# Product sums of the down weights made in device memory: one encoder layer on one core

## The chip, the cores and the metric

One core of a Trainium2 chip runs the kernel. The metric is the device time of one execution in microseconds (us). The engines are TensorE (PE, with its weight loads as PEld), VectorE (DVE), ScalarE (ACT), GpSimd (POOL) and SyncE (SP, which here only issues transfers). Transfers (DMA) run on 16 DMA engines that all the queues share.

## What is computed

One layer of a hybrid encoder over 512 positions of width 1024, float32, cut to what matters:

```python
h  = rmsnorm(x, g_pre_mix)
q, k, v, g, u, sv, a_ret, a_sgu = split(h @ w_in)         # 512, 512 and six times 1024 wide
merged = sigmoid(a_ret) * retention(q, k, v, g) @ w_ret_o \
       + sigmoid(a_sgu) * sgu(u, sv) @ w_sgu_o
x1 = x + rmsnorm(merged @ w_out, g_post_mix)
h2 = rmsnorm(x1, g_pre_ffn)
a, b = split(conv3(h2 @ w_up))                            # 2 x 2816 wide
y  = x1 + rmsnorm((gelu(a) * b) @ w_down, g_post_ffn)     # w_down: 2816 x 1024
```

The last line holds what the change touches: the product with `w_down`, called the down stage, and what follows it, called the tail.

## The kernel before

Every matrix product is done as three matmuls. An operand is split into a high part (a copy on ACT that rounds, line 103, in `copy`) and a low part (source minus high part, a subtraction on DVE, line 123, in `split`), and high x high, high x low and low x high are summed. All weights lie in `wall`, 146 blocks of 128 x 1024, in the order of use. SP loads them into `raw` tiles (four of them, 128 x 1024); split parts go to nine slots of their own. `w_get` takes the next piece of the list `units` and issues loads and splits up to a fixed amount ahead of the matmuls; beyond that, the order on each engine comes from a scheduler that places an instruction when its inputs are due. Each engine runs its own list strictly in order, and an instruction that waits holds all that stands behind it. That holds for transfers too: the engine that issues one waits for its inputs first.

Many products are done in a form of Strassen's scheme, with seven block products in place of eight. They need sums of blocks of the weights and of the other operand. In the down stage, 18 of the 22 row blocks of `w_down` are taken as nine pairs (j = 0 to 8), the other four as they are ("whole"). In a first phase each pair needs four products, with the operand's forms A11, S2, S1 and A22, in a second phase three (A12, S4, S3); each has two token tiles and three matmuls, at line 1406 in `product`. The whole blocks have line 1418. Per pair the weights come from two blocks, a = `wall[i]` and b = `wall[i+1]`, each of two halves C1 and C2 (512 columns), in `w_down`:

- `da` loads a and adds C1 to C2 in place (by DVE at line 236 for even j, by an adding transfer that GpSimd issues, line 234, for odd j). It gives two products.
- `d2` loads b's C2 and adds the sum of `da` (line 244), `d4` loads b's C1 and adds the sum of `d2` (line 247). Each gives one product; their tiles are `dr`, their parts `dt`.
- In the second phase `dc` loads b, and `dd` loads a's C2 and adds b's C2 (line 241).

The operand's forms are made as the gated products `gp` come out of the up stage (`tile_done`), but those of four pairs (`LATE`) only inside the down stage, by `down_sums`, `down_parts` and `down_rest`. Their low parts are made by `split_added`: high part on ACT, its negative on ACT (line 1286), and an adding transfer from GpSimd (line 1287).

In the tail each of four token tiles needs the sum of its squares (ACT, line 1461, into `junk`), a scale from it (DVE at 1472, then GpSimd at 1473), a product with the gain `gpf` (`weighted`, line 1468), a multiply-add with x1 (`rows`, line 1484) and stores (`stored`, line 1477, which takes SP and ACT in turn). For token tiles 0 and 2, `rows_added` (line 1490) scales on DVE and adds x1 by an adding transfer from GpSimd (line 1491) before the store. For tiles 1 and 3 x1 is loaded by SP.

The mixing half of the layer matters here through GpSimd's list: each of four retention heads has a short chain on GpSimd (`rs` line 478, `orstd` line 481, `oshift` line 742), for whose result ACT waits at line 745.

Of the kernel before, what the change touches and what calls it, by code (L numbers as in the profile page):

```python
# [10 lines left out]
F32 = mybir.dt.float32  # L11
# [44 lines left out]
def tile_block(ctx: ExitStack, tc, xT, x, wall, par, cs, wsp, bsp, gpost, gffn, out):  # L56
# [42 lines left out]
    def const(n, shape):  # L99
        return sb.tile(list(shape), F32, tag=n, bufs=1, name=n)  # L100

    def copy(o, i):
        return nc.scalar.activation(out=o, in_=i, func=AF.Copy)  # L103

    def two(t):
        return t.rearrange("p (n c) -> p n c", n=2)
# [8 lines left out]
    def as32(t):  # L115
        return t.bitcast(F32)

    low, w_load = [None], [None]
    HALVES = slice(0, S), slice(S, 2 * S)

    def split(hi, lo, src):
        copy(hi, src)
        low[0] = nc.vector.tensor_sub(lo, src, as32(hi)).ins  # L123


# [6 lines left out]
    while i < NW:  # L132
        pair = [(f, i) for f in FORMS]
        if i == SV0:
            units += [(f, k) for f in ("s11", "sT1", "sT2") for k in range(2)]
            units += [(f, k) for k in range(2) for f in ("s22", "sT3")]
            units += [(f, k) for f in ("s21", "sT4") for k in range(2)]
            i = U0
        elif i == U0:
            us, gs = ([[(f, k + n * m) for f in FORMS] for n in range(KD // 2)] for k, m in ((U0, 2), (GATE0, 4)))  # L140
            ws = [("blk", GATE0 + 4 * (n // 2) + 2 + n % 2) for n in range(KD)]
            for what, n in MIDDLE:
                units += {"W": lambda: ws[n : n + 1], "U1": lambda: us[n][:4], "U2": lambda: us[n][4:],
                          "G1": lambda: gs[n][:4], "G2": lambda: gs[n][4:]}.get(what, list)()
# [77 lines left out]
    def w_down(form, j):  # L222

        i = DOWN0 + 2 * j
        c1, c2 = HALVES

        def load(o, n, c=slice(0, 1024)):
            nc.sync.dma_start(o, wall[i + n, :, c])
            return o

        if form in ("da", "dc"):
            raw = w_raw["a"] = load(raw_tile(), form == "dc")
            if form == "da" and j % 2:
                nc.gpsimd.dma_start(raw[:, c2], wall[i, :, c1], accum_op=ALU.add)
            elif form == "da":
                nc.vector.tensor_add(raw[:, c2], raw[:, c1], raw[:, c2])
            hi, lo = slot("dh", AT_192), slot("dl", AT_192)
        else:
            if form == "dd":
                raw = load(blk(n="dr"), 0, c2)  # L240
                nc.vector.tensor_add(raw, raw, w_raw["a"][:, c2])
            elif form == "d2":
                raw = w_raw["t"] = load(blk(n="dr"), 1, c2)
                nc.vector.tensor_add(raw, w_raw["a"][:, c2], raw)
            else:
                raw = load(blk(n="dr"), 1, c1)
                nc.vector.tensor_add(raw, w_raw["t"], raw)
# [3 lines left out]
        return hi, lo  # L251

    s_sum, s_22 = {}, {}

    def w_sv(form, kp):
# [38 lines left out]
        return w_block(u[1]) if u[0] == "blk" else (w_down if u[0][0] == "d" else w_sv if u[0][0] == "s" else w_form)(*u)  # L294

    def w_size(u):
        return 2 if u[0] in ("blk", "da", "dc") or u[0][0] == "s" else 1

    def w_get(look=LOOK):

# [985 lines left out]
        nc.scalar.activation(out=lo, in_=as32(hi), func=AF.Copy, scale=-1.0)  # L1286
        nc.gpsimd.dma_start(lo, src, accum_op=ALU.add)  # L1287

    def two_parts(t):
        h_, l_ = blk(F32R, "fh"), blk(F32R, "fl")  # L1290
        split_added(h_, l_, t)
        return h_, l_

    firsts, whole, raws = [], [], {}
# [135 lines left out]
    for j in range(DP):  # L1430
        end = j == DP - 1
        if j in LATE:
            n = FORMED + LATE.index(j)
            if n == DP - 1:
                down_sums(n, True)
# [38 lines left out]
        return sc  # L1474

    def stored(n, t, a, b, o):
        (nc.sync, nc.scalar)[n % 2].dma_start(out[t, :, a:b], o)  # L1477

    def rows(t, sc, which, pieces=((0, 512), (512, 1024))):
        for n, (a, b) in enumerate(pieces):  # L1480
# [6 lines left out]
    def rows_added(t, sc, srcs):  # L1487
        for i, src in enumerate(srcs):
            o = blk(n="zs")
            pin(v.scalar_tensor_tensor(out=o, in0=src, scalar=sc, in1=gpf[i], op0=ALU.mult, op1=ALU.mult))  # L1490
            nc.gpsimd.dma_start(o, x1[t][i], accum_op=ALU.add)  # L1491
            stored(i, t, i * S, (i + 1) * S, o)

    yy = halves("e")
    pin = tc.keep_in_program_order
    for j in range(DP):
# [7 lines left out]
            for i in range(2):  # L1504
                nc.gpsimd.dma_start(gpf[i], gffn[None, i * S : (i + 1) * S].to_broadcast([P, S]))
        if j < len(LATE):
            down_rest(FORMED + j)
# [33 lines left out]
    pin(v.tensor_sub(uu[1], m5[1], uu[1]))  # L1541
    square(1, 1, uu[1])
# [140 lines left out]
```

## Time and profile before

| | |
|---|---|
| median of 3 runs | 797.47 us (797.26 to 798.8) |
| profiled execution | 796.85 us, span in the trace 795.1 us |
| granted TensorE clock, mean | 0.989 |
| first matmul of the down stage | 673.6 us |
| first matmul of the whole blocks at the end | 765.25 us |
| last matmul ends | 781.05 us |

The page gives busy times per engine, and the span in 40 slices; the rows of the slices show TensorE at nine tenths or more everywhere but in three places, the second half of the span's last fifth:

```profile
PE   9999999999999999999999999999999999979992
PEclk9999999999999999999999999999999999989997
```

"Idle before" an instruction, in square brackets in a timeline, is the time its engine waited, with what ended the wait. A row of windows has the length, then the busy time of each engine, the granted clock, the DMA engines' busy share and GB/s.

### The profile page before, as it was taken

Reading aid. Unit: us, or ns where it says so; the run is one execution under the profiler, and the core shown is the slowest. Engines: PE = TensorE matmul, PEld = TensorE weight load, DVE = VectorE, ACT = ScalarE, POOL = GpSimd, SP = SyncE. Lnnn points to the kernel's source line nnn. Section 1 sums busy time; section 2 is a strip of 40 time slices with the busy share of each in tenths; the row PEclk is TensorE's granted clock in tenths of the full one; section 3 lists DMA queues with packets and bytes.
Section 4 is the critical chain, followed back from the end, with each engine's and each line's share of the span. In section 5 each row is a group of like instructions: output and inputs, shape, how many; then the busy total and the mean of one; then the engine's idle time right before and its main releaser. Section 6 shows DMA issues by size and latency. Waiting matters only on the chain. (4 is left out here: it accounts for less than half of the span.)

```text
span 795.1 us, 12585 instructions
## 1 busy us (share of the span) xinstructions
PE 772.2 (97%) x4677; PEld 704.8 (89%) x4677; DVE 627.5 (79%) x1050; ACT 492.2 (62%) x884; POOL 117.4 (15%) x147
## 2 busy tenths in 40 slices
PE   9999999999999999999999999999999999979992
PEld 7888999998999999999988999999999998867882
DVE  7467878789789987877765689889999986857764
ACT  7655657788467765644544685657777755646531
POOL 0040010130101102122111200002111102210011
PEclk9999999999999999999999999999999999989997
DMA  8872224462232332333656122335555559886835
GB/s 292 297 221 83 84 76 160 107 153 99 80 111 76 111 128 80 107 106 106 198 197 242 54 80 75 111 113 146 140 146 147 146 164 230 225 219 224 245 93 149
DMA packets 41645, 115.74 MB, mean 146 GB/s; under 512 B 5040, under 2 KB 6960, under 8 KB 41584
## 3 DMA queue, kind: packets, MB, share of 16 engines
q1 hardware_dynamic: 31536, 94.89, 36.2%
q0 software_dynamic: 9184, 18.88, 11.9%
q10 hardware_dynamic: 864, 1.18, 0.4%
q8 instruction: 36, 0.59, 0.3%
q14 instruction: 25, 0.20, 0.1%
HBM read 100.51 MB, written 4.19 MB: 132 GB/s over the span
## 5 line engine op out<-in xcount | busy, mean ns | idle before, releaser
L123 DVE TENSOR_TENSOR wl<-raw,wh 128x1024 fp32r<-128x1024 f32 (+1 forms) x86 | 100.4, 1177 | 59.4 <-issue 20.5
L103 ACT ACTIVATE wf<-raw 128x512 fp32r<-128x512 f32 x140 | 85.9, 625 | 67.0 <-issue 25.5
L945 PE MATMUL ps<-sh,wf 128*128 128x256 f32 x640 | 117.2, 276 | 0.1
L123 DVE TENSOR_TENSOR wf<-raw,wf 128x512 fp32r<-128x512 f32 x140 | 104.9, 755 | 10.1 <-ACT wf L103 9.7
L103 ACT ACTIVATE wh<-raw 128x1024 fp32r<-128x1024 f32 (+2 forms) x90 | 87.1, 981 | 37.3 <-DMA raw<-wall 12.8
L945 PEld LDWEIGHTS ps<-sh,wf 128*128 128x128 f32 x640 | 102.0, 192 | 0.9 <-ACT sig L103 0.5
L320 PE MATMUL ps<-h2h,wh 128*128 128x512 f32 (+1 forms) x256 | 90.6, 354 | 0.0
L321 PE MATMUL ps<-h2l,wh 128*128 128x512 f32 (+1 forms) x256 | 90.4, 353 | 0.0
L322 PE MATMUL ps<-h2h,wl 128*128 128x512 f32 (+1 forms) x256 | 90.4, 353 | 0.0
L945 PE MATMUL ps<-sl,wf 128*128 128x256 f32 x320 | 88.0, 275 | 0.0
L945 PEld LDWEIGHTS ps<-sl,wf 128*128 128x128 f32 x320 | 61.4, 192 | 0.4
L322 PEld LDWEIGHTS ps<-h2h,wl 128*128 128x128 f32 x256 | 48.6, 190 | 5.1
L320 PEld LDWEIGHTS ps<-h2h,wh 128*128 128x128 f32 x256 | 48.6, 190 | 4.5
L321 PEld LDWEIGHTS ps<-h2l,wh 128*128 128x128 f32 x256 | 48.6, 190 | 4.5
L945 PE MATMUL ps<-xh,wf 128*128 128x256 f32 x288 | 52.2, 275 | 0.0
L655 PE MATMUL ps<-wh,xl 128*128 128x512 f32 x128 | 48.5, 379 | 0.0
L654 PE MATMUL ps<-wl,xh 128*128 128x512 f32 x128 | 48.5, 379 | 0.0
L653 PE MATMUL ps<-wh,xh 128*128 128x512 f32 x128 | 48.5, 380 | 0.0
L945 PEld LDWEIGHTS ps<-xh,wf 128*128 128x128 f32 x288 | 45.6, 192 | 0.2
L1287 POOL DMA_DIRECT2D fl<-gp x26 | 23.1, 960 | 125.3 <-DVE wl L123 63.6
L945 PE MATMUL ps<-xl,wf 128*128 128x256 f32 x144 | 39.6, 275 | 0.0
L945 PE MATMUL ps<-h2h,wf 128*128 128x256 f32 x192 | 34.7, 275 | 0.0
(348 smaller groups left out, 2073.1 us busy)
## 6 DMA issues: line engine op xcount, KB each, us to landing
raw<-wall SPq DMA_DIRECT2D x146, 512.0 KB, 3.7
dr<-wall SPq DMA_DIRECT2D x27, 256.0 KB, 6.2
x<-x SPq DMA_DIRECT2D x20, 256.0 KB, 6.3
fl<-gp POOLq DMA_DIRECT2D x18, 256.0 KB, 5.2
fl<-fs POOLq DMA_DIRECT2D x9, 256.0 KB, 4.6
swap<-qkraw POOLq DMA_DIRECT2D x16, 128.0 KB, 4.5
x<-x POOLq DMA_DIRECT2D x8, 256.0 KB, 2.3
xT<-xT SPq DMA_DIRECT2D x7, 256.0 KB, 4.4
```

What stands on the lines that cost most here:

```text
L103: return nc.scalar.activation(out=o, in_=i, func=AF.Copy)
L123: low[0] = nc.vector.tensor_sub(lo, src, as32(hi)).ins
L320: nc.tensor.matmul(o, ah, bh, start=start, stop=False, skip_group_check=skip)
L321: nc.tensor.matmul(o, ah, bl, start=False, stop=False, skip_group_check=skip)
L322: pe_last[0] = nc.tensor.matmul(o, al, bh, start=False, stop=stop, skip_group_check=skip).ins
L653: nc.tensor.matmul(acc[t], xh[k][:, c], turns(wh[:, f]), start=k == 0, stop=False)
L654: nc.tensor.matmul(acc[t], xh[k][:, c], turns(wl[:, f]), start=False, stop=False)
L655: part_end[0] = nc.tensor.matmul(acc[t], xl[k][:, c], turns(wh[:, f]), start=False, stop=k == KD - 1)
L945: self.last = nc.tensor.matmul(o, w_[:, c], a_, start=first and k == n == 0, stop=k == 3 and n == 2, skip_group_check=True,)
L1287: nc.gpsimd.dma_start(lo, src, accum_op=ALU.add)
```

## The change

For each pair j three tensors in device memory are added: t42 (128 x 1024), t1 and t3 (128 x 512). They get the sums that `da`, `d2`, `d4` and `dd` made on chip: t1 = a.C1 + a.C2, t42's C2 = b.C2 + t1, t42's C1 = b.C1 + that, t3 = a.C2 + b.C2. Each begins as a copy from device memory to device memory, issued by ACT (27 in all), to which GpSimd's adding transfers add (36 in all). These 63 operations are issued while other stages run: `copy` counts its calls, and at the counts in `SUMS_AT` it issues the next one behind that copy; an adding transfer waits for that copy, and for the transfers whose results it reads or adds to. Counts 29 to 140 hold the first 48 operations, 312 to 345 the last 15.

`w_down` then only loads: `da` is a.C1 and t1 (two loads into one raw tile), `db` is t42 (one raw tile, two products), `dc` is b as before, `dd` is t3. The 27 sums on DVE and four adding transfers go. In `units`, `d2` and `d4` become one `db` of size 2.

For the late pairs `parted` uses `split`, so their low parts are DVE subtractions (12) in place of 12 negative copies on ACT and 12 adding transfers; these forms are issued after the latest weight split on ACT and DVE (`w_split`). In the tail, tile 0 is done as tile 1 is: `weighted` and `rows`, with x1 loaded by SP; `stored` uses ACT only for tiles above 0, and the second store of tile 2 goes to SP.

```diff
+SUMS_AT = [a + k * (b - a) // n for a, b, n in ((29, 67, 28), (72, 100, 6), (106, 140, 14), (312, 345, 15)) for k in range(n)]
...
     def copy(o, i):
-        return nc.scalar.activation(out=o, in_=i, func=AF.Copy)
+        done = nc.scalar.activation(out=o, in_=i, func=AF.Copy)
+        copies[0] += 1
+        while sums_at and copies[0] >= sums_at[0]:
+            sums_at.pop(0)
+            sums_ops.pop(0)(done.ins)
+        return done
...
+    def sums_copy(j, n):
+        def op(after):
+            i = DOWN0 + 2 * j
+            with tc.issue_after(after):
+                nc.scalar.dma_start(sums[j][n], (wall[i + 1], wall[i, :, C2], wall[i, :, C2])[n])
+        return op
+
+    def sums_add(j, n):
+        def op(after):
+            (t42, t1, t3), i = sums[j], DOWN0 + 2 * j
+            o, src = ((t1, wall[i, :, C1]), (t42[:, C2], t1), (t3, wall[i + 1, :, C2]), (t42[:, C1], t42[:, C2]))[n]
+            add = tc.keep_in_program_order(nc.gpsimd.dma_start(o, src, accum_op=ALU.add))
+            tc.add_manual_dep(
+                add.ins, after.name, mybir.DependencyInfo(mybir.DependencyClass.Sync, mybir.DependencyReason.DATA),
+                reason="paced",
+            )
+        return op
+
+    sums_ops, ended_ = [], []
+    for js in [range(j, min(j + 2, DP)) for j in range(0, DP, 2)]:
+        sums_ops += [sums_copy(j, n) for n in (1, 0) for j in js] + ended_
+        for j in js:
+            sums_ops += [sums_add(j, 0), sums_copy(j, 2)]
+        sums_ops += [sums_add(j, 1) for j in js] + [sums_add(j, 2) for j in js]
+        ended_ = [sums_add(j, 3) for j in js]
+    sums_ops += ended_
...
-                units += [("da", j), ("d2", j), ("d4", j)]
+                units += [("da", j), ("db", j)]
...
     def w_down(form, j):
...
+        t42, t1, t3 = sums[j]
+        if form == "dd":
+            raw = blk(n="dr")
+            nc.sync.dma_start(raw, t3)
             w = slot("dt", 0, 1088)
             lo, hi = w[:, AT_64 : AT_64 + S], w[:, S + AT_192 : 2 * S + AT_192]
+        else:
+            raw = raw_tile()
+            if form == "da":
+                nc.sync.dma_start(raw[:, C1], wall[i, :, C1])
+                nc.sync.dma_start(raw[:, C2], t1)
+            else:
+                nc.sync.dma_start(raw, t42 if form == "db" else wall[i + 1])
+            hi, lo = slot("dh", AT_192), slot("dl", AT_192)
         split(hi, lo, raw)
+        w_split[:] = high[0], low[0]
         return hi, lo
...
     def parted(j, t, *names):
-        h_, l_ = two_parts(t)
+        h_, l_ = two_parts(t, split if j >= FORMED else split_added)
...
-            down_parts(n)
+            with tc.issue_after(w_split[0]), tc.issue_after(w_split[1]):
+                if n == DP - 1:
+                    down_sums(n, True)
+                down_parts(n)
...
-        product(m6, w_get(), 0, "S2", j, last=None)
+        wb = w_get()
+        product(m6, wb, 1, "S2", j, last=None)
...
-        product(m4, w_get(), 0, "A22", j, None)
+        product(m4, wb, 0, "A22", j, None)
...
-        (nc.sync, nc.scalar)[n % 2].dma_start(out[t, :, a:b], o)
+        (nc.sync, nc.scalar)[n % 2 and t > 0].dma_start(out[t, :, a:b], o)
...
-            stored(i, t, i * S, (i + 1) * S, o)
+            nc.sync.dma_start(out[t, :, i * S : (i + 1) * S], o)
...
-        for t in (1, 3):
+        for t in (0, 1, 3):
...
+    weighted(0, 0, m1[0])
...
+    weighted(0, 1, uu[0])
...
-    rows_added(0, s0, (m1[0], uu[0]))
+    rows(0, s0, (0, 1))
```

The change moves instructions in three places. The first is DVE's order inside the first phase of the down stage, before and after (a row has the line, the operation, output and inputs, and the shape; the numbers in names only count tiles). Line 123 of before is line 165 of the change.

```order
L244 TENSOR_TENSOR dr_7666<-raw_7653,dr_7666 128x512
L247 TENSOR_TENSOR dr_7684<-dr_7666,dr_7684 128x512
L244 TENSOR_TENSOR dr_7709<-raw_7696,dr_7709 128x512
L123 TENSOR_TENSOR dl_7657<-raw_7653,dh_7656 128x1024
L247 TENSOR_TENSOR dr_7727<-dr_7709,dr_7727 128x512
L123 TENSOR_TENSOR fa_7792<-gp_7406,fa_7792 128x256
L123 TENSOR_TENSOR dt_7669<-dr_7666,dt_7669 128x512
L123 TENSOR_TENSOR dt_7687<-dr_7684,dt_7687 128x512
```
```order
L165 TENSOR_TENSOR dl_7686<-raw_7683,dh_7685 128x1024
L165 TENSOR_TENSOR fl_7708<-fs_7191,fh_7707 128x512
L165 TENSOR_TENSOR fl_7712<-gp_7186,fh_7711 128x512
L165 TENSOR_TENSOR dl_7719<-raw_7715,dh_7718 128x1024
L165 TENSOR_TENSOR dl_7731<-raw_7728,dh_7730 128x1024
L165 TENSOR_TENSOR dl_7756<-raw_7752,dh_7755 128x1024
```

Before, three sums (L244 and L247, of this pair and the next) stand ahead of the split `dl_7657`; now splits follow one another, with the low parts `fl` of a late form between them.

The second is the end of ACT's order, before and after (line 1461 is 1496 of the change, 1477 is 1512).

```order
L1461 ACTIVATE junk_8329,q_7980<-ps_7533 128x512
L1461 ACTIVATE junk_8352,q_7980<-c_7541 128x512
L1477 DMA out<-zs_8335 128x512
L1461 ACTIVATE junk_8370,q_7981<-ps_7534 128x512
L1461 ACTIVATE junk_8395,q_7981<-c_7542 128x512
L1461 ACTIVATE junk_8416,q_7983<-e_7985 128x256
L1477 DMA out<-zs_8378 128x512
L1461 ACTIVATE junk_8437,q_7983<-e_7985 128x256
```
```order
L1496 ACTIVATE junk_8348,q_8006<-ps_7611 128x512
L1496 ACTIVATE junk_8373,q_8006<-c_7619 128x512
L1496 ACTIVATE junk_8393,q_8007<-ps_7612 128x512
L1496 ACTIVATE junk_8414,q_8007<-c_7620 128x512
L1496 ACTIVATE junk_8435,q_8009<-e_8011 128x256
L1496 ACTIVATE junk_8456,q_8009<-e_8011 128x256
L1512 DMA out<-zs_8420 128x512
L1512 DMA out<-zs_8437 128x256
```

Two stores that stood between the squares now go elsewhere, and the stores that stay on ACT come after the last square.

The third is GpSimd's order around the first retention heads, before and after (478 is 511, 481 is 514, 742 is 775 of the change; line 131 is the adding transfer of `sums_add`).

```order
L478 TENSOR_SCALAR rs_985<-mv 128x4
L481 TENSOR_TENSOR orstd<-rs_985,nhalf 128x4
L742 TENSOR_TENSOR oshift<-oshift,orstd 128x4
L478 TENSOR_SCALAR rs_1273<-mv 128x4
L481 TENSOR_TENSOR orstd<-rs_1273,nhalf 128x4
L742 TENSOR_TENSOR oshift<-oshift,orstd 128x4
```
```order
L511 TENSOR_SCALAR rs_1026<-mv 128x4
L514 TENSOR_TENSOR orstd<-rs_1026,nhalf 128x4
L775 TENSOR_TENSOR oshift<-oshift,orstd 128x4
L131 DMA sum_0_63<-sum_0_63 128x512
L131 DMA sum_0_66<-sum_0_66 128x512
L131 DMA sum_1_70<-wall 128x512
L131 DMA sum_1_73<-wall 128x512
L131 DMA sum_0_69<-sum_1_70 128x512
L131 DMA sum_0_72<-sum_1_73 128x512
L511 TENSOR_SCALAR rs_1325<-mv 128x4
```

Between one head's chain and the next now stand six adding transfers; the last two add results of the two before them (`sum_0` is t42, `sum_1` is t1 and `sum_2` is t3).

More of the change, by code (lines that the diff above doesn't have):

```diff
@@ L100, in const @@
         return sb.tile(list(shape), F32, tag=n, bufs=1, name=n)
+    copies, sums_at = [0], list(SUMS_AT)
     def copy(o, i):
-        return nc.scalar.activation(out=o, in_=i, func=AF.Copy)
+        done = nc.scalar.activation(out=o, in_=i, func=AF.Copy)
[4 more added lines that the diff above has]
+        return done
+    C1, C2 = slice(0, S), slice(S, 2 * S)
+    sums = [[
+        dp_.tile([P, w * S], F32, tag=f"sum{j}_{n}", name=f"sum{j}_{n}") for n, w in enumerate((2, 1, 1))
+    ] for j in range(DP)]
+    def sums_copy(j, n):
[22 more added lines that the diff above has]
+    sums_ops += ended_
     def two(t):
@@ L116, in as32 @@
         return t.bitcast(F32)
-    low, w_load = [None], [None]
+    low, high, w_load = [None], [None], [None]
     HALVES = slice(0, S), slice(S, 2 * S)
     def split(hi, lo, src):
-        copy(hi, src)
+        high[0] = copy(hi, src).ins
         low[0] = nc.vector.tensor_sub(lo, src, as32(hi)).ins
@@ L224, in w_down @@
         i = DOWN0 + 2 * j
[L225 to L247, printed above, removed]
+        t42, t1, t3 = sums[j]
+        if form == "dd":
+            raw = blk(n="dr")
+            nc.sync.dma_start(raw, t3)
             w = slot("dt", 0, 1088)
             lo, hi = w[:, AT_64 : AT_64 + S], w[:, S + AT_192 : 2 * S + AT_192]
+        else:
[6 more added lines that the diff above has]
+            hi, lo = slot("dh", AT_192), slot("dl", AT_192)
         split(hi, lo, raw)
+        w_split[:] = high[0], low[0]
         return hi, lo
+    w_split = []
     s_sum, s_22 = {}, {}
@@ L296, in w_size @@
     def w_size(u):
-        return 2 if u[0] in ("blk", "da", "dc") or u[0][0] == "s" else 1
+        return 2 if u[0] in ("blk", "da", "db", "dc") or u[0][0] == "s" else 1
     def w_get(look=LOOK):
@@ L1287, in split_added, with two_parts @@
         nc.gpsimd.dma_start(lo, src, accum_op=ALU.add)
-    def two_parts(t):
+    def two_parts(t, apart=split_added):
         h_, l_ = blk(F32R, "fh"), blk(F32R, "fl")
-        split_added(h_, l_, t)
+        apart(h_, l_, t)
         return h_, l_
@@ L1433, in tile_block @@
             n = FORMED + LATE.index(j)
-            if n == DP - 1:
-                down_sums(n, True)
-            down_parts(n)
+            with tc.issue_after(w_split[0]), tc.issue_after(w_split[1]):
+                if n == DP - 1:
+                    down_sums(n, True)
+                down_parts(n)
         wa = w_get()
@@ L1506, in tile_block @@
         if j < len(LATE):
-            down_rest(FORMED + j)
+            with tc.issue_after(w_split[0]), tc.issue_after(w_split[1]):
+                down_rest(FORMED + j)
     product(m6, w_get(3.5), 0, "S3", j, None)
```

## The prediction

> **What bounds the kernel now.** I read the page's busy times first, then TensorE's waits, then windows over the down stage, then the timeline inside its longest stall, and last the end of the run.
>
> ```profile
> PE 772.2 (97%) x4677; PEld 704.8 (89%) x4677; DVE 627.5 (79%) x1050; ACT 492.2 (62%) x884; POOL 117.4 (15%) x147
> ```
>
> TensorE bounds the whole: the instruction count on it is unchanged by the edit, so only its idle time, its slow time and what follows its last matmul can be won. The down stage (all matmuls of line 1406) is where it idles. The first fence is TensorE's list of waits from 670 to 766 us (total, times, longest); the second has windows (length, then busy time and instructions of PE, PE's weight load, DVE, ACT, POOL; then granted clock, DMA share, GB/s).
>
> ```profile
> PE ps L1406 <- DVE dl L123: 6.5, 2, 5.0
> PE ps L1406 <- DVE dt L123: 0.6, 1, 0.6
> ```
> ```profile
> 673.60:720.20 46.60, 39.47 (x171) 33.09 (x170) 31.55 (x47) 24.40 (x39) 9.85 (x12) 0.93 0.84 231
> 673.60:765.30 91.70, 84.57 (x380) 72.58 (x379) 63.57 (x87) 50.71 (x76) 13.33 (x16) 0.96 0.78 223
> 706.00:711.00 5.00, 5.00 (x14) 4.07 (x15) 2.84 (x5) 3.58 (x6) 2.01 (x3) 0.59 0.95 194
> ```
>
> How long should this stage take? Three rows of TensorE's timeline (start, duration) give the undisturbed step:
>
> ```profile
> 765.25 0.38 PE L1418 MATMUL ps<-wh,fh 128*128 128x512 f32 x1
> ...
> 778.20 0.27 PE L1418 MATMUL ps<-wh,fh 128*128 128x256 f32 x1
> ...
> 780.77 0.28 PE L1418 MATMUL ps<-wh,fl 128*128 128x256 f32 x1
> ```
>
> Between the first two start 60 matmuls 512 wide (five groups of 12), so 12.95 / 60 = 0.216 us each. The down stage has nine pairs with 24 such matmuls in its first phase (216) and 18 in its second (162): 378 x 0.2158 = 81.6 us, where 673.60 to 765.25 is 91.65. So **10.1 us** are lost, nearly all in the first phase: its first 46.6 us hold 171 matmuls where 216 fit, and 45 x 0.216 is 9.7. Of the loss, 7.1 us are the waits above. Behind the longest the clock was 0.59 for 5 us, in which 14 matmuls ran that need 3.0 us at the full step: another 2.0. The last microsecond is spread.
>
> Why the split comes late is in the timeline of DVE, SP's queue and TensorE:
>
> ```profile
> 696.51 9.58 SPq L228 DMA_DIRECT2D raw<-wall  x2
> ...
> 702.22 0.69 DVE L247 TENSOR_TENSOR dr<-dr,dr 128x512 f32<-128x512 f32 x1 [1.73 <-DMA dr<-wall]
> ...
> 704.52 1.22 DVE L123 TENSOR_TENSOR dl<-raw,dh 128x1024 fp32r<-128x1024 f32 x1
> ...
> 705.79 0.79 PE L1406 MATMUL ps<-dl,fa 128*128 128x512 f32 x1 [5.00 <-DVE dl L123]
> ```
>
> The low part that TensorE awaits is one 1.22 us subtraction. In DVE's order it stands behind sums (L244, L247, L236) of later blocks, and these wait for loads. Those loads share the DMA engines with GpSimd's adding transfers: the two queues below took 36.2% of 795.1 us for 94.89 MB, 3.03 us of all engines per MB, and 11.9% for 18.88 MB, 5.01 per MB.
>
> ```profile
> q1 hardware_dynamic: 31536, 94.89, 36.2%
> q0 software_dynamic: 9184, 18.88, 11.9%
> ```
>
> First phase, in need: 9 x 1.05 MB of loads, 28.6 us, and 12 adding transfers of 0.26 MB (4 for odd pairs, 8 for late forms), 15.8 us: 44.4 of 46.6 us. That leaves no room to catch up; the first window's 0.84 agrees.
>
> **The down stage after the change.** All 27 DVE sums and the 4 adding transfers go; the loads stay 1.05 MB a pair; the 8 adding transfers of late forms become DVE subtractions. So DMA need falls to 28.6 of 46.6 us, 61%. Groups and issues from 670 to 765 us price the rest (busy, mean ns; KB each, us to landing):
>
> ```profile
> L123 DVE TENSOR_TENSOR dl<-raw,dh 128x1024 fp32r<-128x1024 f32 x17 | 20.7, 1220 | 1.2 <-ACT dh L103 1.2
> L123 DVE TENSOR_TENSOR dt<-dr,dt 128x512 fp32r<-128x512 f32 x27 | 18.0, 688 | 1.7 <-ACT dt L103 1.5
> L103 ACT ACTIVATE dh<-raw 128x1024 fp32r<-128x1024 f32 x17 | 17.8, 1047 | 6.3 <-PE ps L1406 6.3
> ...
> raw<-wall SPq DMA_DIRECT2D x17, 512.0 KB, 4.6
> ...
> fl<-gp POOLq DMA_DIRECT2D x8, 256.0 KB, 7.5
> ```
>
> DVE in the first phase: 18 splits x 1.22 + 8 low parts x 0.69 (the price of dt, same shape) = 27.5 of 46.6 us, none of them behind a load of a later block's sum. ACT: 18 x 1.05 and 8 half-width copies of about 0.62 (from the 1.05), 24 us; its 12 negative copies are gone. Neither is near its limit. New is that the second block, formerly two tiles elsewhere, now takes a raw tile: two raw tiles per pair of 5.2 us (24 x 0.216), out of four, so a tile must turn round in 10.4 us. Its round is 4.6 load + 1.05 + 1.22 = 6.9, which leaves 3.5 for queueing. In the second phase the third sums come as 0.26 MB loads and nine additions go; nothing waited there for long, so I count no gain. I take 9.6 of the 10.1 us, leaving about one wait such as the 0.6 us one. Bounds: 4.5 (rival B) to 10.1.
>
> Where I trust the 2.0 us of half clock to go: the Trainium skill ("TensorE: Matmul & The Clock Gate", Part 1: The HAM clock gate) has the clock halved after an idle window of about 3.4 us. By that rule it vanishes as soon as the 5.0 us wait is shorter than this; the trace shows one such case only, so the row carries the sum and the rule does not.
>
> **The tail.** Rows of ACT and DVE after 778 us, and one of the chain of waits:
>
> ```profile
> 778.39 0.35 ACTq L1477 DMA_DIRECT2D out<-zs  x1
> 778.78 0.60 ACT L1461 ACTIVATE junk<-ps 128x512 f32<-128x512 f32 x1 [4.11 <-PE ps L1418]
> ...
> 779.50 0.69 DVE L1468 TENSOR_TENSOR zs<-ps,gpf 128x512 f32<-128x512 f32 x1 [4.64 <-ACT junk L1461]
> ...
> 781.43 0.69 DVE L1541 TENSOR_TENSOR c<-ps,c 128x512 f32<-128x512 f32 x1
> ...
> 785.17 0.42 DVE L1549 TENSOR_TENSOR e<-ps,e 128x256 f32<-128x256 f32 x1
> ...
> 788.15 0.35 ACTq L1477 DMA_DIRECT2D out<-zs  x1
> 788.60 0.42 ACT L1461 ACTIVATE junk<-e 128x256 f32<-128x256 f32 x1 [3.93 <-DMA zs<-x]
> ...
> 789.14 0.16 DVE L1472 SCALAR_TENSOR_TENSOR qs<-q 128x1 f32<-128x1 f32 x1 [2.43 <-ACT junk L1461]
> ```
> ```profile
> 782.04 6.08 DMA zs<-x
> ```
>
> TensorE ends at 781.05; the run lasts 14.0 us more, to 795.1. Twice ACT holds a store that waits for GpSimd's adding transfer, with a square queued behind it. The square at 778.78 has had its input since about 775.6 (48 matmuls after 765.25); DVE's whole order waits behind it. The one at 788.60 has its input from 785.6. In the new order no store stands ahead of a square. Then: square at 775.8, product 776.4, the two rows of token tile 0 (0.74 each), and L1541's subtraction when its matmuls end (778.4) and DVE reads them: 778.6, 2.8 us sooner. The final piece follows at the same spacing: 785.17 - 2.8 = 782.4, square 0.5 later, its scale about 0.95 after that: 783.85 in place of 789.14. From there on nothing changes (5.9 us to the end). Gain **5.3 us**. Bounds: 3.9, the second hold alone, and 6.2, if the last subtraction starts right behind TensorE's end. The two added loads of x1 for tile 0 go out on SP after the last weights, 0.52 MB x 3.03 = 1.6 us of a DMA that then only has stores.
>
> **What the sums cost.** 27 copies and 36 adding transfers from device memory to device memory, 9.44 MB each way of counting. By what stands next to them in ACT's order, 23 copies (8.13 MB) and 25 adds (6.55 MB) run at about 52 to 215 us, 4 (1.31) and 11 (2.88) at 479 to 515.
>
> ```profile
> 52.00:215.00 163.00, 163.00 (x918) 146.82 (x917) 132.72 (x230) 110.02 (x189) 18.49 (x30) 1.00 0.39 112
> 479.00:515.00 36.00, 36.00 (x232) 33.37 (x231) 33.75 (x53) 22.16 (x37) 0.00 (x0) 1.00 0.32 103
> ```
>
> No row shows a transfer with both ends in device memory. Low bound, the prices above: 8.13 x 3.03 + 6.55 x 5.01 = 57.4 us on top of 163 x 0.39 = 63.6, 74% of the window; high bound, twice that: 110%. The late one: 18.4 on 11.5 of 36 us (83%), or 36.9 (134%). I take the low price, as each row read or wrote device memory at one end already, and count zero: TensorE is busy 163.00 and 36.00 us there, and its weights come ahead of need. The tightest I found, a split and its first use:
>
> ```profile
> 489.12 1.22 DVE L123 TENSOR_TENSOR wl<-raw,wh 128x1024 fp32r<-128x1024 f32 x1
> ...
> 495.10 0.38 PE L320 MATMUL ps<-h2h,wh 128*128 128x512 f32 x1
> ```
>
> That is 4.8 us ahead. At the high bound the late window would be 12 us short: some 7 us on TensorE; the early one 16 us short over 163 us, of which part is absorbed. Issuing costs 27 x 0.35 (the rows of ACT's queue above) = 9.5 us of ACT, which is busy 110 of 163 us, and 36 x 0.96 of POOL, 18 of 163; the work of both hides under TensorE's.
>
> ```profile
> L1287 POOL DMA_DIRECT2D fl<-gp x26 | 23.1, 960 | 125.3 <-DVE wl L123 63.6
> ```
>
> **The sum.** Against the profiled execution, 796.85 us (1.75 around its span, 0.62 under the median): 796.85 - 9.6 - 5.3 = 781.95; against the median, 782.6. I say **782.5**.
>
> **Rivals.**
>
> *B: the stall moves to the raw tiles.* For: SP's row above took 9.58 us over two raw loads, so it already waited for tiles, and now two per pair are wanted. Against: those tiles were held by the late splits, and the round needs 6.9 of 10.4 us. If the 6.5 us of waits for dl shrink only to 4.5 without half clock, and one us stays spread, the stage wins 4.6 and the run ends at 797.47 - 4.6 - 5.3 = 787.6.
>
> *D: the sums crowd the loads.* For: the upper bounds over 100%. Against: the window has 0.39 and 0.32 now. It costs 1 to 8 us: 784 to 790.
>
> *C: slower than before, by GpSimd's order.* POOL also makes four scales of the retention heads, and ACT's next copies stand behind them:
>
> ```profile
> POOL rs L478 <- DVE mv L735: 80.0, 4, 39.4
> ...
> ACT o L745 <- POOL oshift L742: 4.7, 3, 2.4
> ```
> ```profile
> 93.72 0.53 POOL L478 TENSOR_SCALAR rs<-mv 128x4 f32<-128x4 f32 x1 [39.38 <-DVE mv L735]
> ...
> 116.11 0.20 POOL L478 TENSOR_SCALAR rs<-mv 128x4 f32<-128x4 f32 x1 [20.46 <-DVE mv L735]
> ```
>
> Six adds now stand between the first two, and the last pair waits for the landing of the pair before. The interval is 22.4 us; with 6 x 0.96 of issue, 1.7 of own work and 4.8 of lead, it breaks when a landing takes over about 20 us. Each further us makes each of four heads late by one, so 24 us would eat 15 and give 798, 26 us 806. Against: adds land in 7.5 us in the crowded stage. The Trainium skill ("DMA: Bandwidth & Descriptors", Anatomy of one DMA) says that the completion of a transfer can take surprisingly long when the target is device memory, which is just this kind. In this trace plain stores to device memory land in 2.1 us, the row below, and no row adds into it, so neither is settled.
>
> ```profile
> out<-zs ACTq DMA_DIRECT2D x3, 256.0 KB, 2.1
> ```
>
> **Chances and range.** Both gains nearly whole: 0.62 (own range 780 to 785). B 0.17, D 0.12, C 0.07, and 0.02 that crowding and stall together leave the time where it was. Range 779.5, a little under the sum with all bounds high (797.47 - 10.1 - 6.2 = 781.2, less a us or two of second-phase gains that I counted at nothing), to 790.5, which holds B and most of D. A measurement of this kernel tells 0.2%, 1.6 us, from no change: faster 0.91, same 0.02, slower 0.07.
>
> **What would show it.** Right: TensorE's waits at the down stage under 1.5 us and its 378 matmuls in 82 to 83 us at clock 1.00; DMA share there near 0.6; the run ends under 9 us after the last matmul; TensorE stays fully busy in both windows of the sums. Wrong, B: waits for dl remain, with ACT's high part waiting for a raw load and SP for a tile. Wrong, D: TensorE idles at 479 to 515 us behind a load. Wrong, C: ACT waits for POOL's oshift by over 10 us a head, with adding transfers ahead of it.

## The result

The changed kernel takes 784.3 us (median of 5 runs, 782.61 to 784.8) where the kernel before took 797.26 beside it (5 runs, 797.01 to 798.8): a ratio of 0.983, 95% interval 0.9816 to 0.9845, 13.0 us. The profiled execution took 782.61 us, the fastest of the five, with a span of 780.7. A second set, with a profile of its own, gave 784.36 (4 runs) and 0.9837 (0.9824 to 0.9851).

| piece of the span | before | changed, first profile | changed, second profile |
|---|---|---|---|
| start to the first matmul of the down stage | 673.6 | 675.2 | 677.0 |
| down stage, 378 matmuls | 91.65 | 81.6 | 81.6 |
| whole blocks, to the end of the last matmul | 15.8 | 15.8 | 15.8 |
| last matmul to the end | 14.0 | 8.1 | 8.2 |
| span | 795.1 | 780.7 | 782.6 |

Two pieces got shorter by 10.1 and 5.9 us, and everything ahead of them got longer by 1.6 to 3.4. First the busy times on the page of the changed kernel, then TensorE's waits over the whole run (total, times, longest): no wait of the down stage is left in them.

```profile
PE 770.9 (99%) x4677; PEld 705.2 (90%) x4677; DVE 617.1 (79%) x1023; ACT 484.2 (62%) x863; POOL 131.2 (17%) x165
```
```profile
PE ps L978 <- ACT c L106: 0.8, 1, 0.8
PE ps L454 <- PEq L1711: 0.8, 1, 0.8
```

Windows over the first 46.6 us of the down stage and over the whole stage (length; busy time and instructions of PE, PE's weight load, DVE, ACT, POOL; clock, DMA share, GB/s):

```profile
675.20:721.80 46.60, 46.60 (x217) 40.87 (x216) 29.36 (x32) 24.46 (x31) 0.00 (x0) 1.00 0.66 217
675.20:756.80 81.60, 81.60 (x380) 71.55 (x379) 51.94 (x59) 43.72 (x57) 0.00 (x0) 1.00 0.63 211
```

Where 171 matmuls ran before, the first window now holds 217 (216 fit, one is cut by its edge), at the full clock, with DVE at 29 and ACT at 24 of 46.6 us and the DMA engines at two thirds. The waits have turned round: over 673 to 757 us it is the splits that wait for TensorE to free their slots.

```profile
ACT dh L106 <- PE ps L1439: 14.3, 9, 2.9
DVE dl L165 <- PE ps L1439: 11.8, 7, 2.7
```

The tail, by ACT and DVE (timeline rows: start, duration, engine, line):

```profile
767.34 0.60 ACT L1496 ACTIVATE junk<-ps 128x512 f32<-128x512 f32 x1 [1.14 <-PE ps L1451]
...
769.99 0.68 DVE L1579 TENSOR_TENSOR c<-ps,c 128x512 f32<-128x512 f32 x1
...
774.24 0.42 ACT L1496 ACTIVATE junk<-e 128x256 f32<-128x256 f32 x1 [1.01 <-DVE e L1587]
...
775.18 0.15 DVE L1507 SCALAR_TENSOR_TENSOR qs<-q 128x1 f32<-128x1 f32 x1
```

TensorE's last matmul ends at 772.57. The square on `ps` now waits for TensorE and not behind a store, L1579 (1541 before) starts 2.6 us ahead of that end, where it stood 0.4 us behind it, and the last scale comes 2.6 us after it in place of 8.1.

Most of what became longer in this profile shows near 500 us. The window 479 to 515 us of the changed kernel, then a piece of the chain of waits there:

```profile
479.00:515.00 36.00, 35.18 (x220) 32.08 (x219) 32.57 (x52) 21.24 (x36) 5.73 (x7) 1.00 0.71 171
```
```profile
494.46 8.07 DMA raw<-wall
...
505.57 3.12 PE ps L978 x24
```

And the same moment on ACT, in the kernel before and in the changed one, where the last row is TensorE's:

```profile
498.50 0.63 ACT L103 ACTIVATE wf<-raw 128x512 fp32r<-128x512 f32 x1 [2.14 <-DMA raw<-wall]
...
502.42 0.37 ACT L103 ACTIVATE c<-ps 128x256 f32<-128x256 f32 x1
```
```profile
502.55 1.15 ACT L106 ACTIVATE wf<-raw 128x512 fp32r<-128x512 f32 x2 [5.75 <-DMA raw<-wall]
...
505.15 0.36 ACT L106 ACTIVATE c<-ps 128x256 f32<-128x256 f32 x1
...
505.57 0.38 PE L978 MATMUL ps<-h2h,wf 128*128 128x256 f32 x1 [0.82 <-ACT c L106]
```

The DMA share has gone from 0.32 to 0.71, and one load of weights took 8.07 us (4.4 before). ACT waited 5.75 us for it in place of 2.14. Behind that wait in ACT's order stands the copy `c` out of a tile of results `ps`, for which TensorE waits. Before, the copy ended 1.4 us ahead of the matmuls that need it; now TensorE idles 0.82 us for it. At the first matmul of a like group on either side, TensorE was 0.4 us behind the kernel before at 490 us and 1.6 us behind at 509 us: 1.2 us were lost here. In the second profile it was 1.9 us behind at 491 us and 3.5 at 510 us. (The numbers of matmuls in such windows don't measure a loss, since matmuls of two widths alternate here: another kernel below has 224 in place of 232 with TensorE busy throughout.)

### The profile page after: what moved, and what is told of

The parts are those of the page before. It is cut to its first block, busy times and chain, and to the rows that moved or that the text cites. A ratio compares the mean times of both kernels' runs of the same rounds, so it can differ in the third digit from the quotient of the medians.

```text
span 780.7 us, 12620 instructions
## 1 busy us (share of the span) xinstructions
PE 770.9 (99%) x4677; PEld 705.2 (90%) x4677; DVE 617.1 (79%) x1023; ACT 484.2 (62%) x863; POOL 131.2 (17%) x165
## 3 DMA queue, kind: packets, MB, share of 16 engines
q0 software_dynamic: 11776, 23.60, 16.7%
q10 hardware_dynamic: 3456, 10.09, 3.8%
## 4 chain that ended last, share of the span: by engine, by line
PE 93%; DVE 4%; DMA 1%; issue 1%; ACT 0%; POOLq 0%; DVEq 0%; SPq 0%; ACTq 0%
PE ps L978 23%; PE ps L353 11%; PE ps L354 11%; PE ps L355 11%; PE ps L1439 10%; PE ps L807 5%; PE ps L686 4%; PE ps L687 4%; PE ps L688 4%; PE ps L1451 2%; PE ps L1160 2%; PE ps L1159 2%; PE ps L1161 2%; DMA raw<-wall 1%; PE ps L1049 1%; PE ps L472 1%
## 5 line engine op out<-in xcount | busy, mean ns | idle before, releaser
L165 DVE TENSOR_TENSOR wf<-raw,wf 128x512 fp32r<-128x512 f32 x140 | 106.1, 765 | 10.5 <-ACT wf L106 10.1
L165 DVE TENSOR_TENSOR dl<-raw,dh 128x1024 fp32r<-128x1024 f32 x27 | 33.0, 1225 | 21.7 <-PE ps L1439 11.8
L106 ACT ACTIVATE dh<-raw 128x1024 fp32r<-128x1024 f32 x27 | 28.4, 1052 | 22.4 <-PE ps L1439 14.3
```

The source lines that it names most:

```text
L106: done = nc.scalar.activation(out=o, in_=i, func=AF.Copy)
```

## Experiments

The kernel before ran beside each set; its medians there were 795.88, 795.28 and 797.05 us, so runs of different sets are compared by their ratios.

### The tail alone, and the traffic alone

The first kernel is the kernel before with only the change's edits of the tail (x1 of tile 0 loaded by SP, `weighted` and `rows` for it, the two stores on SP):

```diff
-        (nc.sync, nc.scalar)[n % 2].dma_start(out[t, :, a:b], o)
+        (nc.sync, nc.scalar)[n % 2 and t > 0].dma_start(out[t, :, a:b], o)
...
-    rows_added(0, s0, (m1[0], uu[0]))
+    rows(0, s0, (0, 1))
```

> The kernel before with the change's tail alone: tile 0 by VectorE with x1 loaded by SP, and the two stores moved to SP. Theory (a square on ScalarE waits behind a store that waits for an adding transfer): the span ends 5 to 6 us earlier, 791.3 to 792.3 us against 797.3, all of it behind TensorE's last matmul (8.0 to 8.8 us to the end in place of 14.0), while the down stage keeps its 91.6 us. Rival (the tail gained only because the down stage before it had freed VectorE and the DMA engines): under 3 us, above 794.3.

Measured: 791.63 us (6 runs), 0.9946 (0.9923 to 0.9968), 4.3 us less. The profiled execution, 792.6, has its last matmul start at 782.04 and end at 782.32, and lasts 8.5 us more:

```profile
782.04 0.28 PE L1418 MATMUL ps<-wh,fl 128*128 128x256 f32 x1
...
784.08 0.42 ACT L1461 ACTIVATE junk<-e 128x256 f32<-128x256 f32 x1 [1.11 <-DVE e L1551]
```

So 5.5 us of the tail come without the down stage's part of the change. The total is 1 us short of that: in this profile the down stage took 93.3 us, with a wait of 1.5 us more than before; its stalls differ between executions. The theory holds for the tail; the total fell short of its 5 to 6 us, though the interval (2.5 to 6.1 us) holds them.

The second is the kernel before with the 63 sum operations added and nothing reading them:

> The kernel before with the 63 transfers of the sums added, whose results nothing reads. Theory (the late 15 of them crowd the weight loads at 479 to 515 us, nothing else): 1 to 3.5 us slower, 798.3 to 800.8, with TensorE idle 0.5 to 2 us near 505 us and the DMA share of 52 to 215 us raised from 0.39 to about 0.77 at no cost. Rival 1 (the traffic costs nothing; the changed kernel lost its 1.6 us before the down stage otherwise): 797.0 to 797.7. Rival 2 (the traffic also costs beside the early weights): over 801.

Measured: 799.9 us (10 runs), 1.0039 (1.0022 to 1.0055), 4.0 us more by medians, 3.1 by the ratio. The down stage begins at 675.6 us (2.0 late) and takes 93.2 us with its own stalls as before, and near 500 us as much is lost (1.4 us):

```profile
PE ps L1448 <- DVE dl L165: 6.4, 2, 5.4
PE ps L987 <- ACT c L106: 0.9, 1, 0.9
PE ps L363 <- DVE st L165: 0.9, 1, 0.9
```

The traffic costs 2 to 4 us: more than nothing (rival 1), and not only at 500 us, as the theory had it. The last row, a wait for a part of the retention's state at 167 us, lies in the early stretch.

### What made the stall: the sums on VectorE or the adding transfers?

One kernel leaves out VectorE's sums (all 32 of them, 23 in the first phase and the 9 of `dd`), the other the adding transfers:

```diff
-            elif form == "da":
-                nc.vector.tensor_add(raw[:, c2], raw[:, c1], raw[:, c2])
...
-                nc.vector.tensor_add(raw, raw, w_raw["a"][:, c2])
...
-                nc.vector.tensor_add(raw, w_raw["a"][:, c2], raw)
...
-                nc.vector.tensor_add(raw, w_raw["t"], raw)
```

> The kernel before with the 23 sums that VectorE makes in the down stage left out (the weights there are then not the sums); its adding transfers stay. Order theory (the splits are late since they stand behind sums that wait for loads on VectorE): waits for splits under 1.5 us in all, the stage in 82 to 84 us in place of 91.65, the run at 788 to 790 us. Crowding theory (the adding transfers fill the DMA engines, 44 of 46.6 us in the first phase, so the loads are late for whoever needs them): waits of 3 us or more remain, the stage takes 86 to 92 us, the run 791 to 797.

```diff
-                nc.gpsimd.dma_start(raw[:, c2], wall[i, :, c1], accum_op=ALU.add)
...
-        nc.gpsimd.dma_start(lo, src, accum_op=ALU.add)
+        if add:
+            nc.gpsimd.dma_start(lo, src, accum_op=ALU.add)
```

> The kernel before with the 16 adding transfers of the down stage left out (the weights of odd pairs lack a sum, the low parts of the late forms lack their source); VectorE's sums stay. Crowding theory: the loads come in time, the stage takes 82 to 84 us, the run 788 to 790. Order theory: sums on VectorE still hold splits, waits of 3 us or more remain, the stage takes 86 to 92 us, the run 791 to 797.

Measured, one run each: 785.71 us without VectorE's sums, 788.33 without the adding transfers. Windows over the same 46.6 us, of the first kernel and then of the second:

```profile
673.60:720.20 46.60, 46.60 (x217) 40.81 (x216) 26.15 (x36) 30.59 (x48) 9.89 (x12) 1.00 0.91 267
```
```profile
673.60:720.20 46.60, 45.05 (x208) 38.85 (x207) 39.42 (x57) 28.59 (x45) 0.00 (x0) 1.00 0.62 214
```

Without the sums, the DMA engines are busier than before (0.91 against 0.84), and transfers land later; the list of issues of that kernel from 670 to 765 us has them (KB each, us to landing; 6.4 and 7.5 in the kernel before):

```profile
dr<-wall SPq DMA_DIRECT2D x21, 256.0 KB, 8.6
fl<-gp POOLq DMA_DIRECT2D x8, 256.0 KB, 9.0
```

Yet TensorE loses nothing, and the whole stage takes 81.6 us. Nearly full DMA engines stall nothing here as long as no instruction queue passes the delay on. Without the adding transfers loads land in time (512 KB in 3.3 us, not 4.6), and the sums on VectorE still cost something: 208 matmuls, 83.7 us for the stage. So the stall needed VectorE's sums to happen at all, and the crowded DMA engines set most of its size. Each theory came out about right for its own kernel (a stage of 81.6 and of 83.7 us) and predicted a remainder of 4 us or more for the other's; the order theory was wrong on that, and the crowding theory wrong altogether in the first kernel.

Leaving the sums out takes 23 x 0.69 = 15.9 us of work from VectorE's first phase as well as the waiting, and this run alone can't tell the two apart. VectorE's list of waits in the kernel before (673 to 766 us) shows the waiting, 10.6 us before sums of the first phase:

```profile
DVE raw L236 <- DMA raw<-wall: 3.8, 2, 3.1
DVE dr L247 <- DMA dr<-wall: 3.5, 3, 1.7
DVE dr L244 <- DMA dr<-wall: 3.3, 2, 2.3
```

Without the adding transfers such waits come to 4.2 us. All the work of the sums is then still there, and 2.1 of the 10.1 us stay lost: most of the stall follows the waiting and not the work.

### Which part of the change does it in the down stage?

The kernel before with the late forms' low parts by VectorE (issued behind the latest weight split, as in the change) and nothing else; then the changed kernel with those low parts by adding transfers again. The first one's edit at the main place, which the second takes back:

```diff
-        h_, l_ = two_parts(t)
+        h_, l_ = two_parts(t, split if j >= FORMED else split_added)
```

> The kernel before with one part of the change alone: the late forms' low parts by VectorE (12 subtractions for 12 adding transfers and 12 negative copies), sums and tail as before. Theory after the first four runs (the stall needs both, VectorE's sums and the adding transfers; either one taken away frees the stage): the stage in 82 to 85 us, the run 8 to 10 us under the kernel before. Rival (VectorE is now full: 9 x 1.22 + 18 x 0.69 + 23 x 0.69 + 8 x 0.69 = 44.8 of 46.6 us in the first phase): the stage keeps 88 us or more, the run at most 4 us under, or slower.

> The changed kernel with the late forms' low parts again by adding transfers; sums and tail as changed. Theory (VectorE has no sum that waits, so the 8 adding transfers of the first phase hurt nobody): same as the changed kernel within 0.5 us, the stage at 81.6 to 82.2 us. Rival (39 of 46.6 us of DMA need are too much for raw tiles that now turn twice per pair): 2 to 6 us slower than the changed kernel.

Measured: 787.86 us for the late forms alone (4 runs), 0.9908 (0.9882 to 0.9934), 7.4 us less; and 784.31 with them undone (4 runs, 783.47 to 786.43), 0.9863 (0.9837 to 0.9889). Windows over the first 46.6 us, of the one and of the other:

```profile
673.60:720.20 46.60, 43.72 (x196) 36.12 (x195) 38.09 (x56) 20.92 (x32) 2.89 (x4) 1.00 0.65 208
```
```profile
673.60:720.20 46.60, 46.60 (x217) 40.80 (x217) 24.81 (x25) 28.32 (x37) 7.96 (x10) 1.00 0.87 265
```

Late forms alone free the DMA engines (0.65), but put 12 more instructions on a VectorE that still has its 32 sums: short waits stay (the longest 1.1 us, with the granted clock at 1.00), and the profiled stage takes 88.0 us. That execution, 790.0 us, was the slowest of the four. The gain fell between the two expectations. With the sums made in device memory, the stage does not need the late forms' part: the DMA engines are back at 0.87 and it takes 81.6 us. So in the changed kernel the sums alone are enough for the down stage's gain. By the ratios this kernel is 2 to 3 us behind the changed one, with intervals that overlap; a gain of that size elsewhere is neither shown nor excluded.

If the late forms get 7 us without any traffic, do they and the tail together do as well?

> Late forms by VectorE and the changed tail together, without any of the sums in device memory. If the theory of e4 holds: 13.5 to 16 us under the kernel before, as good as the changed kernel or up to 2 us better, since the 63 transfers cost nothing here. If the rival of e4 holds: 6 to 10 us under, 4 us or more behind the changed kernel.

Measured: 784.96 us (4 runs), 0.9869 (0.984 to 0.9898), 10.3 us less. The profiled stage took 85.8 us, the tail 8.3, and the down stage began at 673.0, with no traffic ahead of it. The expectation was missed, between its two cases. By the ratios it is 3 us behind the changed kernel, though the intervals touch.

### Where the sums are made

The last 15 operations are moved from copies 312 to 345 to copies 345 to 420, beside the late up stage, or to 145 to 295, beside the gates; and all 63 are packed into copies 29 to 140:

```diff
-SUMS_AT = [... for a, b, n in ((29, 67, 28), (72, 100, 6), (106, 140, 14), (312, 345, 15)) for k in range(n)]
+SUMS_AT = [... for a, b, n in ((29, 67, 28), (72, 100, 6), (106, 140, 14), (345, 420, 15)) for k in range(n)]
```

> The changed kernel with its last 15 sum operations at copies 345 to 420 (about 520 to 605 us) in place of 312 to 345 (479 to 515 us). Theory (they cost 1 to 3 us where the weights come just in time, as the 8.07 us load of a raw tile at 494 us shows): 1 to 3 us better than the changed kernel, the first matmul of the down stage back at 673.6 us. Rival (the loss only moves with them, since the loads there use 0.57 of the DMA engines already): the same or slower than the changed kernel.

Measured: 782.31 us (4 runs), 0.9832 (0.9809 to 0.9854), in a set without the changed kernel; by the ratio that is no better than the changed kernel's 0.983. It was run again beside the changed kernel, with the other two places:

> The changed kernel once more, as the measure for the three kernels beside it: 0.982 to 0.987 of the kernel before, with its first down matmul 1 to 2 us later than before.

> The changed kernel with its last 15 sum operations at copies 345 to 420, beside the changed kernel on one chip. Theory (these 15 cost 1 to 3 us at 479 to 515 us and nothing later): 1 to 2.3 us under the changed kernel. Rival (the first look at it was another chip's doing): within 0.5 us.

> The changed kernel with its last 15 sum operations at copies 145 to 295 (about 215 to 405 us), where GpSimd makes sums of the gates' weights that ScalarE waits for. Theory (an adding transfer holds GpSimd's own work only while it waits for the landing before it, 5 to 6 us, and the lead covers that): as the kernel with the last 15 at 520 to 605 us, within 1 us. Rival (GpSimd's order decides): 2 to 8 us slower than the changed kernel, with TensorE idle behind ScalarE's copies of GpSimd's sums.

> The changed kernel with all 63 sum operations spread evenly over copies 29 to 140 (about 57 to 212 us). By the trace of the changed kernel the copies take 2.9 us of the DMA engines per MB and the sums' adds about 6.3, so this stretch would hold 63.6 + 89 = 153 of 163 us. Theory (under the limit, leads absorb it): no loss beyond the kernel with the last 15 at 520 to 605 us, or up to 2 us. Rival 1 (crowding): weights late, 3 to 10 us slower than the changed kernel, with TensorE idle behind loads before 215 us. Rival 2 (GpSimd's order): 5 us or more slower, with ScalarE waiting over 10 us per head for oshift.

| kernel | median us | runs | ratio to before, interval |
|---|---|---|---|
| changed | 784.36 | 783.86 to 784.68 | 0.9837 (0.9824 to 0.9851) |
| last 15 at copies 345 to 420 | 782.79 | 781.27 to 783.01 | 0.9809 (0.9796 to 0.9823) |
| last 15 at copies 145 to 295 | 782.66 | 782.27 to 782.68 | 0.9815 (0.9802 to 0.9829) |
| all 63 at copies 29 to 140 | 789.39 | 788.25 to 790.1 | 0.99 (0.9886 to 0.9913) |

The two moves win 1.6 and 1.7 us, with no run of either as slow as the fastest of the changed kernel; which of them is faster can't be told. (The changed kernel's first down matmul came 3.4 us late here and not 1 to 2.) In the window that lost time TensorE is fully busy again; it, and the one that took the transfers, in the kernel with copies 345 to 420:

```profile
479.00:515.00 36.00, 36.00 (x224) 33.13 (x223) 33.75 (x53) 21.45 (x36) 0.00 (x0) 1.00 0.29 90
515.00:605.00 90.00, 90.00 (x596) 83.89 (x595) 83.06 (x140) 65.15 (x121) 22.15 (x26) 1.00 0.71 174
```

The second carries the same DMA share, 0.71, as the lossy window did, and TensorE loses nothing in it. So the share alone doesn't decide. What differs is the room: in the kernel before, ScalarE waits for no load between 515 and 605 us, where it waited 2.14 us for one at 498. With the transfers there it waits 1.2 us at most (1.7 in the other profile), and no copy that TensorE needs comes late. The version at copies 145 to 295 also answers the rival about GpSimd: its adds stand among sums that ScalarE waits for, and no loss came of it.

Packed into the early stretch, the same work costs 5 us over the changed kernel. The window 165 to 200 us of that kernel, two rows of its issues from 160 to 200 us (the loads, and the adding transfers to the sums of `sv`'s weights), the piece of its chain of waits, and the wait of TensorE:

```profile
165.00:200.00 35.00, 29.03 (x158) 25.52 (x157) 23.72 (x39) 22.63 (x39) 11.41 (x16) 0.95 1.01 249
```
```profile
raw<-wall SPq DMA_DIRECT2D x6, 512.0 KB, 11.6
...
sb<-wall POOLq DMA_DIRECT2D x4, 256.0 KB, 14.7
```
```profile
172.13 22.50 DMA sb<-wall
```
```profile
PE ps L879 <- ACT gh L106: 5.1, 1, 5.1
```

The DMA engines are full (1.01; in the changed kernel they were at 0.90 over the same stretch, with TensorE busy throughout). An adding transfer of the kernel's own, issued among those of the sums on GpSimd's queue, lands 22.5 us after its issue; the median of these four is 14.7 us against 7.7 in the changed kernel. ScalarE's splits wait for it, the copy `gh` stands behind them, TensorE idles 5.1 us, and the granted clock is 0.66 over the 5 us behind that. Plain loads of 512 KB are late in this stretch too: 11.6 us against 5.9 in the changed kernel. ScalarE's wait for `oshift` was 6.5 us in all, less than in the changed kernel (7.7), so GpSimd's own instructions were not late. This is rival 1, the crowding, in its mechanism and in its size; only the transfer that TensorE waited for was an adding one and not a plain load.

## Why the prediction was right, and where it was off

**The sum.** 782.5 us was forecast, from -9.6 and -5.3 and nothing for the sums. Measured by the two profiles: -10.1, -5.9 (or -5.8), and +1.6 (or +3.4); by the median 784.3. The likeliest case came true, in the upper part of its own range of 780 to 785, with a share of rival D in it. There is some luck in that: the two gains were 1.1 us larger than forecast and hid part of the sums' cost. With both as forecast the median would have been 785.4, just outside. Of the signs that were named, those of the down stage and the tail all showed (the stage even took less, 81.6 us and not 82 to 83); TensorE fully busy in both windows of the sums did not (35.18 of 36 us in the late one).

**The down stage.** The stall was taken whole, 10.1 us, and with it the half clock. The prediction left 0.5 us for a remaining wait; there is none. The needs it worked out for the first phase came close: VectorE 27.5 us against 29.4 measured, ScalarE 24 against 24.5, DMA share 0.61 against 0.66. Of its reasoning, the step with VectorE's order (a split that stands behind sums of later blocks) is what the runs bear out. The step "That leaves no room to catch up", which made the DMA need of 44.4 in 46.6 us a cause of its own, does not hold: with the sums gone and the engines at 0.91 TensorE lost nothing. Together with the sums it does count: without the adding transfers 8.0 of the 10.1 us went. And the count of sums was wrong: the change takes 32 from VectorE, not 27. (27 is the net fall of its instructions, 1050 to 1023.) No term of the sum hung on it. The row of 40 slices, too, has TensorE under nine tenths in two slices and not in three: 696 to 716 us, the long stall, and the last.

**Rival B** (raw tiles) did not show: SP waits for tiles, but the splits wait for TensorE and not the reverse.

**The tail.** The mechanism was right, at 5.3 against 5.9 us. L1541's subtraction came 2.6 us ahead of the end of TensorE (forecast 2.5), the last piece (L1549, now L1587) 1.2 us behind it (1.35) with its square 0.5 us later, the last scale 2.6 us behind it (2.8). What the term missed is mostly what was taken as unchanged: from the last scale to the end it is 5.5 us, where it was 5.9.

**The sums' cost** is the term that was mis-sized: zero, "its weights come ahead of need". The engines' time was about as forecast (the share rose by 0.38 x 163 = 62 us where the low bound said 57, and by 0.39 x 36 = 14 against 18), so the low price was the right choice. What failed was the step from there to no loss. The prediction measured the lead from a split to its own matmuls, 4.8 us at the tightest. It overlooked the row at 498.50 us: ScalarE had no lead there, it already waited 2.14 us for that load, and the copy `c` that TensorE needs stood behind it with 1.4 us to spare. The load then took 8.07 us in place of 4.4. So the loss has the pattern of the down stage's stall, on another engine: an instruction that waits for a transfer stands ahead of one that TensorE needs. Moving the 15 operations gave 1.6 us back, and the first down matmul then stood at 673.9 us in one profile and 675.6 in another; the rest, 0.3 to 2.0 us, belongs to the early 48. Part of it is a wait of TensorE for `st` near 167 us: 0.4 to 1.3 us in seven of the eight profiles with these transfers, absent from the six without. Why it comes was not tested.

**Rival C**, the slower case, was looked for where it would be: ScalarE waited 7.7 us for `oshift` in place of 4.7, in three waits, and 9.8 us in the second profile. The two profiles with the longest wait for `st` (1.3 us) are also those with the longest single wait for `oshift` (4.3 and 4.4 us, 1.5 before), so a small share of rival C may lie in the early cost; that is not shown. The adds into device memory landed no later than those into on-chip tiles; the issues of the changed kernel from 40 to 230 us:

```profile
sum<-wall ACTq DMA_DIRECT2D x8, 512.0 KB, 4.7
...
sum<-wall POOLq DMA_DIRECT2D x13, 256.0 KB, 6.0
sum<-sum POOLq DMA_DIRECT2D x12, 256.0 KB, 5.4
...
sb<-wall POOLq DMA_DIRECT2D x4, 256.0 KB, 7.7
```

The rule of the Trainium skill ("DMA: Bandwidth & Descriptors", Anatomy of one DMA), by which completion can be surprisingly long for device memory, did not price this kernel: 5.4 and 6.0 us against 5.2 for the kernel's own adds before. In the full stretch of the packed version adds were late into both kinds of memory alike (medians of 14.1 to 14.7 us).

## What to carry to other kernels

An operation that waits for a transfer should not stand, in an in-order queue, ahead of one that the critical engine needs. With the sums out of VectorE's queue, DMA engines at 0.91 cost nothing in the down stage; at 1.01, in the packed version, they did cost. When work is moved beside other stages, look for the place by what already waits for its loads there, and for what stands behind that wait, not by the free share of the DMA engines: 0.71 cost over 1 us at one place and nothing at another. And count a shift that is called free against the smallest lead in every queue that leads to the critical engine, since one late load is enough.

## What the runs showed of the hardware

Plain copies with both ends in device memory cost what loads do; adding transfers there cost somewhat more than the other transfers of GpSimd's queue. The two queues that carry them in the changed kernel give the prices:

```profile
q0 software_dynamic: 11776, 23.60, 16.7%
q10 hardware_dynamic: 3456, 10.09, 3.8%
```

Plain copies: 3.8% of 780.7 us for 10.09 MB, 2.9 us of all engines per MB, as loads cost 3.0 before. Adds: 130.4 us for 23.60 MB. Of these, 14.16 MB were there before at 5.01 each, which leaves 59.5 us for the 9.44 MB of the sums, 6.3 per MB. That is an estimate, since it takes the price of the others as unchanged; in the kernel before it was 4.3 over 40 to 230 us and 5.3 over 670 to 765 us.

Behind TensorE's long waits the granted clock was low for about 5 us: 0.59 behind 5.0 us in the kernel before, 0.53 behind 4.5 us in the kernel with the tail alone, 0.66 behind 5.1 us in the packed one. Behind a wait of 1.75 us in the second of them it was 1.00.
